# Eighteen places instead of twelve in the ring of the experts' loads, finer last loads of w_down, and the final scaling divided among three engines

## The chip, the cores and the metric

One core of a Trainium2 chip runs the kernel. The metric is device microseconds of one execution. The engines are named as in the profile: PE (matrix products), DVE (elementwise, from SBUF and PSUM), ACT (scaling and functions), POOL (elementwise on SBUF) and SP (only issues transfers). ACT and POOL can issue transfers too. All transfers run on the same 16 DMA engines of the core.

## What is computed

Two transformer blocks run one after the other on 256 tokens of width 1024, in 32-bit floats. The first holds a mixer of window attention, a recurrent scan and memory attention, and a convolutional feed-forward layer. The second holds two kinds of attention, and then a mixture of 32 experts, whose output is added to x before a last normalization:

```python
h2 = rmsnorm(x, norm2_g[l]) * (1.0 + sc2[:, None, :]) + sh2[:, None, :]
y_ffn = hierarchical_moe(h2, w_group[l], b_group[l], w_expert[l], b_expert[l],
                         w_gate[l], w_up[l], w_down[l])
x = x + g2[:, None, :] * y_ffn
...
return rmsnorm(x, final_g)
```

Each token goes to one of 4 groups and to 2 of the 8 experts of that group. An expert computes `silu(t @ w_gate) * (t @ w_up) @ w_down`, with w_gate and w_up of 1024 x 512 and w_down of 512 x 1024. Each of these matrices is 2 MB, so that the weights of all experts are 192 MB, and all of them are read.

## The kernel before

Everything up to the experts (called the front here) takes weights through a ring of six places of 1 MB each (`raw0` to `raw5`, 128 partitions x 2048 floats). `slot("raw")` (line 209) hands out the next place in turn. Each arriving MB is split into a high and a low part in a second ring `hi`, and PE multiplies with both parts.

The experts' stage begins at line 1431. Its ring has twelve places: two in the part `spare` of the long-lived tile `kept`, the six `raw`, and four new tiles `eraw0` to `eraw3` (`NMORE = 4`). `load` (line 1474) fills one place by one transfer of 1 MB, issued by SP (line 1479): four of the eight row groups of a gate or up matrix of one expert, or two of the four row groups of a down matrix. A load is behind all loads of the front in SP's queue (`issue_after(ahead)`), and it waits until the place's earlier content has been read. For an `eraw` tile that is the content of whichever tiles lay on the same bytes of SBUF before. Addresses are given out by an allocator that sees all tiles of the program, and a scheduler fixes the order of the instructions of each engine.

The loop runs over 8 groups of 4 experts (`EG = 4`). For each group, `times` loads four places for the first half of w_gate, multiplies, and does the same for the second half; then come both halves of w_up. `gather` (line 1442) builds the one-hot matrix `OH` and picks the tokens of the group into `XG` on PE (line 1454). `hidden` and `down` of the group before are done between the halves of the gate product. A group needs 24 loads, so that the whole stage has 192. In `times` the loop over the four row groups is outside of the loop over the experts, so that the four places of a half are all in use until its last products.

`down` (line 1504) loads two halves of w_down for four experts, and adds the products in two PSUM banks, `pd[0]` and `pd[1]` (columns 0 to 511 and 512 to 1023, line 1512). Then, for each half of the columns: DVE scales (`ye`, line 1518), ACT and DVE split into `yh` and `yl` (lines 1519 and 1520), PE brings the rows back to their tokens (lines 1523 and 1524), and DVE adds them to x (line 1525, one operand in PSUM and one in SBUF).

Three more transfers matter. The row `g2` is read after the loads of the front (line 234). The last gain goes to `row1` of `kept` (line 1584). `row0` of `kept` holds `g1`, which line 1288 reads for the last time ahead of the routing; `stage`, which lies right behind `row0`, is last used in the front.

`finish` (line 1586) makes the sums of squares (`squares`; three of four on ACT, the last on DVE, line 265), the reciprocal root on DVE (`token_rstd`, nine small instructions, lines 279 and 250 to 257), and then four products of 128 x 512 on DVE (line 1595), each followed by a store from SP (line 1596). After it stands a branch over `overflow`, which runs only where an expert has more than 32 tokens.

Of the kernel before, what the change touches and what calls it, by code (L numbers as in the profile page):

```python
# [9 lines left out]
F32 = mybir.dt.float32  # L10
# [4 lines left out]
AF = mybir.ActivationFunctionType  # L15
OP = mybir.AluOpType
# [4 lines left out]
D = 1024  # L21
NE = 32
CAP = 32
EG = 4
OC = 64
NMORE = 4
NRAW = 6
NHIS = 4
NEAR = 3
# [145 lines left out]
def _body(ctx, tc, nc, I, O, dbg):  # L175
    V, A, P, SY, G = nc.vector, nc.scalar, nc.tensor, nc.sync, nc.gpsimd

    def pool(stack, name, bufs=1, **kw):
        if kw.get("space") != bass.MemoryType.DRAM:
            kw["reuse_waits"] = "tile"  # L180
        return stack.enter_context(tc.tile_pool(name=name, bufs=bufs, **kw))
# [10 lines left out]
    kept = keep.tile([128, nk], F32, name="kept")  # L192
# [3 lines left out]
    x = pool(stx, "xs").tile([128, 2, D], F32, name="x")  # L196
# [12 lines left out]
    def slot(k):  # L209
        ring[k].append(ring[k].pop(0))  # L210
        return ring[k][-1]
# [29 lines left out]
    def pt(name="pt"):  # L241
        return psm.tile([128, 512], F32, name=name, tag="ps")

    def at(name="at"):
        return acc.tile([128, 512], F32, name=name, tag="acc")
# [13 lines left out]
    def squares(ssq, src, n):  # L259

        for t in range(2):
            junk = small.tile([128, 512], F32, name="junk", tag="junk", bufs=2)
            z = src[:, t, n * 512:n * 512 + 512]
            if n and t and SQ:
                V.scalar_tensor_tensor(junk, z, 1.0, z, op0=OP.mult, op1=OP.mult, accum_out=ssq[:, n, t:t + 1])
            else:
                A.activation(junk, z, AF.Square, accum_out=ssq[:, n, t:t + 1])

    def square_sums():
        return small.tile([128, 2, 2], F32, name="ssq", tag="ssq")  # L270
# [59 lines left out]
    def piece(srcs, J, behind=None, rest=(), first=0):  # L330


        w = sum(s.shape[-1] for s in srcs)
        out, n = [], max(1, 1024 // w)
        m = 2048 // (n * w) * n
        for i0 in range(first, J, m):
            i1 = min(J, i0 + m)
            rv = slot("raw")[:, :(i1 - i0) * w].rearrange("p (j f) -> p j f", f=w)
            c = 0
            for s in srcs:  # L340
                turn["load"] = SY.dma_start(rv[:, :, c:c + s.shape[-1]], s[:, i0:i1, :]).ins
                if behind is not None:
                    hold(turn["load"], behind)
                c += s.shape[-1]
            for j0 in range(i0, i1, n):
                k = min(n, i1 - j0)
                hl = slot("hi")
                hv, lv = (z[:, :k * w].rearrange("p (j f) -> p j f", j=k) for z in (hl[:, :1024], hl[:, 1024:]))
                rh = rv[:, j0 - i0:j0 - i0 + k, :]
                A.activation(hv, rh, AF.Copy)  # L350
                (G if j0 in rest else V).tensor_tensor(lv, rh, hv.bitcast(F32), op=OP.subtract)  # L351
                out.append((j0, k, hv, lv))
        return out
# [10 lines left out]
    def cols(w, a, b):  # L364
        return w.rearrange("(j p) n -> p j n", p=128)[:, :, a:b]
# [35 lines left out]
    def head_rstd(pl, src, n, tag):  # L401

        sq = pl.tile([128, n * 64], F32, name="hsq", tag="hsq", bufs=2)
        A.activation(sq, src, AF.Square)
        ss = small.tile([128, n], F32, name="hss", tag=f"hss{n}")
        V.tensor_reduce(ss, sq.rearrange("p (h d) -> p h d", d=64), axis=AX.X, op=OP.add)
        V.tensor_scalar(ss, ss, 1.0 / 64, 1e-6, op0=OP.mult, op1=OP.add)
        r = small.tile([128, n], F32, name=tag, tag=tag)
        rsqrt(r, ss, n)
        return r  # L410
# [54 lines left out]
    lo = ks["row1"][0]  # L465
# [29 lines left out]
    for c0, n in ((8, 2), (0, 4), (4, 4)):  # L495
        ws = piece([cols(w_in, 640 + c0 * 128, 640 + (c0 + n) * 128)], 8)
        for k, p in enumerate(feature_major(xs, ws, n)):
# [3 lines left out]
                                   op0=OP.mult, op1=OP.add)  # L501
# [6 lines left out]
    ws = piece([cols(w_in, 0, 512)], 8)  # L508
    for t, p in enumerate(token_major(xs, ws, 512)):
        r = head_rstd(pp, p, 8, "qkr")  # L510
# [3 lines left out]
    ws = piece([cols(w_in, 512, 640), cols(w_in, 1920, 2176)], 8)  # L514
    for t, p in enumerate(token_major(xs, ws, 384)):
        A.activation(va[:, t, :], p[:, :128], AF.Copy)
        r = head_rstd(pp, p[:, 128:384], 4, "qmr")
# [285 lines left out]
    ws = piece([cols(I["w_mem_kv"][0], 0, 512)], 8)  # L803
    for t, p in enumerate(token_major(ms_, ws, 512)):
        A.activation(mv[:, t, :], p[:, 256:], AF.Copy)
        r = head_rstd(pp, p[:, :256], 4, "mkr")
# [141 lines left out]
    ssq = square_sums()  # L948
    for n in range(2):
        ws = piece([cols(I["w_out"][0], n * 512, n * 512 + 512)], 8, behind=rw["near"])  # L950
# [21 lines left out]
    def conv(p, f):  # L972
        u = fp.tile([128, T], F32, name="conv", tag="conv", bufs=4)
        A.activation(u, p[:, :T], AF.Identity, scale=cw[:, 2, f:f + 1], bias=R("conv_b", f))
        V.scalar_tensor_tensor(u[:, 1:], p[:, :T - 1], cw[:, 1, f:f + 1], u[:, 1:], op0=OP.mult, op1=OP.add)
        V.scalar_tensor_tensor(u[:, 2:], p[:, :T - 2], cw[:, 0, f:f + 1], u[:, 2:], op0=OP.mult, op1=OP.add)
        return u

    for i in range(FB // 2):
        ws = piece([cols(w_up, 256 * i, 256 * i + 256), cols(w_up, 2816 + 256 * i, 2816 + 256 * i + 256)], 8)  # L980
        ps = [p[:, k * T:(k + 1) * T] for p in feature_major(xs, ws, 4, alloc=pt, each=2)
              for k in range(2)]
        for k in range(2):
            f = 2 * i + k
            g, v = conv(ps[k], f), conv(ps[2 + k], FB + f)
# [44 lines left out]
    ssq = square_sums()  # L1030
    for n in range(2):
        dst = None
        for off, J in ((0, 8), (8, 8), (16, 6)):
            ws = piece([w_down[off * 128:(off + J) * 128, n * 512:n * 512 + 512].rearrange("(j p) n -> p j n", p=128)], J)
# [217 lines left out]
    for m, _ in enumerate(project(1, "w_proj_diff_2")):  # L1252
        for k in range(0, 4, 2):
# [4 lines left out]
                                   op0=OP.mult, op1=OP.subtract)  # L1258
# [20 lines left out]
    ssq = square_sums()  # L1279
    for n in range(2):  # L1280
        ws = piece([cols(I["w_out_2"][0], n * 512, n * 512 + 512)], 8)
# [3 lines left out]
        for t, p in enumerate(ps):  # L1285
            f = slice(n * 512, n * 512 + 512)
            y = ip.tile([128, 512], F32, name="yo", tag="yo", bufs=2)
# [5 lines left out]
    ahead = turn["load"]  # L1293
# [77 lines left out]
    ep = pool(est0, "moe0")  # L1371
# [6 lines left out]
    r = token_rstd(x, ssq)  # L1378
# [39 lines left out]
    for t in range(2):  # L1418
# [3 lines left out]
    p = pt()  # L1422
# [8 lines left out]
    ep = pool(est, "moe")  # L1431
    lo = ks["spare"][0]
    ring["raw"] = ([kept[:, a:a + 2048] for a in (lo, lo + 2048)] + ring["raw"]
                   + [ep.tile([128, 2048], F32, name=f"eraw{i}") for i in range(NMORE)])
    wg, wu, wd = I["w_gate_2"][0], I["w_up_2"][0], I["w_down_2"][0]
    slots = C("slots")[:, :CAP]
    EC = EG * CAP
# [1 line left out]
    def quarter(e):  # L1439
        return slice(e * CAP, e * CAP + CAP)  # L1440
# [34 lines left out]
    def load(w, e, k0, n, k, d):  # L1475

        rv = slot("raw")[:, :n * d].rearrange("p (j f) -> p j f", f=d)
        with tc.issue_after(ahead):
            SY.dma_start(rv, w[e].rearrange("(p j) f -> p j f", j=k)[:, k0:k0 + n, :])
        return rv  # L1480
# [23 lines left out]
    def down(g, hT, back, iv):  # L1504
        pd = [at("pd") for _ in range(2)]
        for half in range(2):
            ws = [load(wd, EG * g + e, 2 * half, 2, 4, D) for e in range(EG)]
            for i in range(2):
                q = 2 * half + i
                for n in range(2):  # L1510
                    for e in range(EG):
                        P.matmul(pd[n][quarter(e), :], hT[:, q, quarter(e)], ws[e][:, i, n * 512:n * 512 + 512],  # L1512
                                 start=q == 0, stop=q == 3)
        for n in range(2):
            f = slice(n * 512, n * 512 + 512)
            y = ep.tile([128, 512], F32, name="ye", tag="ye", bufs=2)
            yh, yl = (ep.tile([128, 512], F32R, name=k, tag=k, bufs=2) for k in ("yh", "yl"))
            V.scalar_tensor_tensor(y, pd[n], iv, g2[:, f], op0=OP.mult, op1=OP.mult)  # L1518
            A.activation(yh, y, AF.Copy)  # L1519
            V.tensor_tensor(yl, y, yh.bitcast(F32), op=OP.subtract)  # L1520
            for t in range(2):
                p, b = pt(), back[:, t * 128:(t + 1) * 128]
                P.matmul(p, b, yh, start=True, stop=False)  # L1523
                P.matmul(p, b, yl, start=False, stop=True)  # L1524
                V.tensor_tensor(x[:, t, f], p, x[:, t, f], op=OP.add)
# [34 lines left out]
    NG = NE // EG  # L1560
# [22 lines left out]
    fg = part["row1"]  # L1583
    SY.dma_start(fg, I["final_g_2"][None, :].to_broadcast([128, D]))

    def finish(pl):
        ssq = square_sums()
        for n in range(2):
            squares(ssq, x, n)
        r = token_rstd(None, ssq)  # L1590
        for t in range(2):
            for n in range(2):
                f = slice(n * 512, n * 512 + 512)
                y = pl.tile([128, 512], F32, name="y", tag="y", bufs=4)
                V.scalar_tensor_tensor(y, x[:, t, f], r[:, t:t + 1], fg[:, f], op0=OP.mult, op1=OP.mult)
                SY.dma_start(O["out"][0, t * 128:(t + 1) * 128, f], y)

    finish(ep)
    ring["raw"] = list(raws)
    est.close()  # L1600
# [38 lines left out]
```

## Time and profile before

| | us |
|---|---|
| three timed runs, median (lowest to highest) | 1160.4 (1159.4 to 1164.57) |
| the profiled execution, own time | 1152.61 |
| its span, first to last instruction | 1150.6 |

| engine | busy us | share of the span |
|---|---|---|
| PE | 1008.5 | 88% |
| DVE | 486.8 | 42% |
| ACT | 363.1 | 32% |
| POOL | 32.5 | 3% |

The page of the profile gives the transfers' share and rate in 40 slices of 28.8 us. In slices 0 to 23 the rate is between 1 and 359 GB/s; from slice 24 on it is 420 to 422 GB/s in every slice but the last. The chain of work that ended last is put down to DMA for 28% of the span, to PE for 14% and to DVE for 2%. All times below are microseconds from the first instruction of the profiled execution.

### The profile page before, as it was taken

To read this page: it belongs to the slowest core of one execution; us is meant where nothing else is said; L and a number is where in the kernel's file an instruction comes from. 1 tells how busy PE (TensorE), PEld (TensorE's weight loads), DVE (VectorE), ACT (ScalarE), POOL (GpSimd) and SP (SyncE) were. 2 spreads that over 40 slices of the span, in tenths; PEclk is the share of its full clock that TensorE was granted. 3 is DMA by queue.
4 is the path that set the end of the run, shared out by engine and by line. 5 is a ranking of instruction groups with operands and counts; after the bars stand their busy time and mean duration, and the time that the engine had idled before them with its cause. 6 is when DMAs were issued, how large, how long until landed. Compare 5 with 4: busy or idle time off the path is not lost. (4 is left out here: it accounts for less than half of the span.)

```text
span 1150.6 us, 14934 instructions
## 1 busy us (share of the span) xinstructions
PE 1008.5 (88%) x6028; PEld 678.8 (59%) x6028; DVE 486.8 (42%) x1023; ACT 363.1 (32%) x647; POOL 32.5 (3%) x43
## 2 busy tenths in 40 slices
PE   5998989989999998999999988878787887878774
PEld 4984767659999986777999762423233231414121
DVE  5686533467888846547676720202020200101023
ACT  5553544146666644445554310000000000001001
POOL 0000010100000000211000000000000000000000
PEclk9999989999999998999999988999899998999888
DMA  9706375864567565353348549999999999999993
GB/s 359 252 1 186 140 303 174 286 204 134 184 183 226 183 220 183 121 172 111 119 139 327 203 176 420 421 421 421 421 421 421 422 421 420 422 420 421 421 420 140
DMA packets 94200, 317.49 MB, mean 276 GB/s; under 512 B 10730, under 2 KB 38048, under 8 KB 66348
## 3 DMA queue, kind: packets, MB, share of 16 engines
q1 hardware_dynamic: 90476, 291.25, 66.1%
q0 software_dynamic: 3648, 25.22, 5.9%
q8 instruction: 49, 0.80, 0.3%
q14 instruction: 27, 0.22, 0.1%
HBM read 315.36 MB, written 2.26 MB: 276 GB/s over the span
## 5 line engine op out<-in xcount | busy, mean ns | idle before, releaser
L351 DVE TENSOR_TENSOR hi<-raw,hi 128x1024 fp32r<-128x1024 f32 (+1 forms) x152 | 184.9, 1219 | 116.1 <-ACT hi L350 115.5
L350 ACT ACTIVATE hi<-raw 128x1024 fp32r<-128x1024 f32 (+1 forms) x152 | 159.6, 1054 | 165.6 <-PE at L380 87.1
L1518 DVE SCALAR_TENSOR_TENSOR ye<-pd,iv,kept 128x512 f32<-128x512 f32 x16 | 12.0, 750 | 281.0 <-PE pd L1512 280.1
L1512 PE MATMUL pd<-raw,hT 128*32 128x512 f32 x368 | 101.5, 599 | 19.4 <-DMA raw<-in_w_down_dram 18.7
L395 PE MATMUL pt<-fh,hi 128*128 128x256 f32 x352 | 99.7, 283 | 0.0
L397 PE MATMUL pt<-fh,hi 128*128 128x256 f32 x352 | 99.6, 283 | 0.0
L396 PE MATMUL pt<-fl,hi 128*128 128x256 f32 x352 | 99.6, 283 | 0.0
L1488 PE MATMUL pg<-eraw,XG 128*32 128x512 f32 x224 | 56.1, 771 | 26.0 <-DMA eraw<-in_w_gate_dram 26.0
L1512 PEld LDWEIGHTS pd<-raw,hT 128*32 128x32 f32 x368 | 23.4, 109 | 93.6 <-DMA raw<-in_w_down_dram 50.2
L1488 PE MATMUL pg<-raw,XG 128*32 128x512 f32 x272 | 58.3, 676 | 14.4 <-DMA raw<-in_w_gate_dram 14.4
L396 PEld LDWEIGHTS pt<-fl,hi 128*128 128x128 f32 x352 | 67.6, 192 | 0.0
L395 PEld LDWEIGHTS pt<-fh,hi 128*128 128x128 f32 x352 | 67.6, 192 | 0.0
L397 PEld LDWEIGHTS pt<-fh,hi 128*128 128x128 f32 x352 | 67.6, 192 | 0.0
L1454 PEld LDWEIGHTS pt<-OH,xa 128*128 128x128 f32 x256 | 62.0, 334 | 5.9 <-issue 5.0
L1454 PE MATMUL pt<-OH,xa 128*128 128x128 f32 x256 | 64.5, 409 | 0.7 <-DVE OH L1447 0.7
L1519 ACT ACTIVATE yh<-ye 128x512 fp32r<-128x512 f32 x16 | 10.1, 631 | 143.6 <-DVE ye L1518 143.6
L1494 DVE TENSOR_TENSOR h<-h,pu 128x512 f32<-128x512 f32 x8 | 5.5, 689 | 114.9 <-PE pu L1488 114.9
L1488 PEld LDWEIGHTS pg<-eraw,XG 128*32 128x32 f32 x224 | 11.3, 133 | 64.7 <-DMA eraw<-in_w_gate_dram 45.6
L1493 ACT ACTIVATE h<-pg 128x512 f32<-128x512 f32 x8 | 4.8, 597 | 128.8 <-PE pg L1488 128.8
L1488 PE MATMUL pu<-eraw,XG 128*32 128x512 f32 x256 | 43.6, 596 | 0.8 <-DMA eraw<-in_w_up_dram 0.8
L1512 PE MATMUL pd<-kept,hT 128*32 128x512 f32 x112 | 36.6, 605 | 4.8 <-ACT h L1493 4.8
L1488 PEld LDWEIGHTS pg<-raw,XG 128*32 128x32 f32 x272 | 12.2, 121 | 45.1 <-DMA raw<-in_w_gate_dram 26.2
(465 smaller groups left out, 2008.8 us busy)
## 6 DMA issues: line engine op xcount, KB each, us to landing
raw<-in_w_down_dram SPq DMA_DIRECT2D x56, 1024.0 KB, 19.8
raw<-in_w_gate_dram SPq DMA_DIRECT2D x34, 1024.0 KB, 19.5
eraw<-in_w_up_dram SPq DMA_DIRECT2D x32, 1024.0 KB, 19.6
eraw<-in_w_gate_dram SPq DMA_DIRECT2D x28, 1024.0 KB, 16.5
raw<-in_w_in_dram SPq DMA_DIRECT2D x27, 1024.0 KB, 5.1
kept<-in_w_ada_dram POOLq DMA_DIRECT2D x24, 1024.0 KB, 6.3
raw<-in_w_up_dram SPq DMA_DIRECT2D x44, 512.0 KB, 4.6
kept<-in_w_up_dram SPq DMA_DIRECT2D x16, 1024.0 KB, 19.6
```

The lines of the kernel that those rows point to most:

```text
L350: A.activation(hv, rh, AF.Copy)
L351: (G if j0 in rest else V).tensor_tensor(lv, rh, hv.bitcast(F32), op=OP.subtract)
L395: P.matmul(d, wh[:, j, f], xh[xj], start=i == 0 and j == 0 and k % each == 0, stop=False)
L396: P.matmul(d, wh[:, j, f], xl[xj], start=False, stop=False)
L397: P.matmul(d, wl[:, j, f], xh[xj], start=False, stop=i == len(ws) - 1 and j == n - 1 and k % each == each - 1)
L1454: P.matmul(pv[:, j, :], by_j(xa[:, t])[:, jj * 4 + j, :], OH[:, t], start=t == 0, stop=t == 1)
L1488: P.matmul(p[quarter(e), :], XG[:, jj, quarter(e)], ws[e][:, j, :], start=jj == 0, stop=jj == 7)
L1493: A.activation(h, pg, AF.Silu)
L1494: V.tensor_tensor(h, h, pu, op=OP.mult)
L1512: P.matmul(pd[n][quarter(e), :], hT[:, q, quarter(e)], ws[e][:, i, n * 512:n * 512 + 512], start=q == 0, stop=q == 3)
L1518: V.scalar_tensor_tensor(y, pd[n], iv, g2[:, f], op0=OP.mult, op1=OP.mult)
L1519: A.activation(yh, y, AF.Copy)
```

## The change

- `NMORE` goes from 4 to 9, so that there are five more `eraw` tiles, and the 1024 + 1024 floats of `row0` and `stage` become an eighteenth place, at the end of the ring. The ring's order is: two of `spare`, six `raw`, nine `eraw`, one of `row0` and `stage`.
- The last half of w_down of the last group comes in 12 transfers in place of 4: for each of the four experts 512 KB (its third row group), then for each 256 KB (the first 512 columns of its fourth row group), then for each the other 256 KB. Rows in memory are 4 KB and 2 KB long there, in place of 8 KB.
- In `finish`, POOL multiplies x with the last gain, in four pieces, while the sums of squares are made. Once the reciprocal root is there, DVE scales the two pieces of tokens 0 to 127 and ACT those of tokens 128 to 255, and SP and ACT each issue two of the four stores.

```diff
-NMORE = 4
+NMORE = 9
...
     ring["raw"] = ([kept[:, a:a + 2048] for a in (lo, lo + 2048)] + ring["raw"]
-                   + [ep.tile([128, 2048], F32, name=f"eraw{i}") for i in range(NMORE)])
+                   + [ep.tile([128, 2048], F32, name=f"eraw{i}") for i in range(NMORE)] + [kept[:, lo - 2048:lo]])
...
-            ws = [load(wd, EG * g + e, 2 * half, 2, 4, D) for e in range(EG)]
+            if g == NG - 1 and half:
+
+                ws = [slot("raw").rearrange("p (j f) -> p j f", f=D) for e in range(EG)]
+                for i, f in ((0, slice(0, D)), (1, slice(0, 512)), (1, slice(512, D))):
+                    for e in range(EG):
+                        with tc.issue_after(ahead):
+                            SY.dma_start(ws[e][:, i, f], wd[EG * g + e].rearrange("(p j) f -> p j f", j=4)[:, 2 + i, f])
+            else:
+                ws = [load(wd, EG * g + e, 2 * half, 2, 4, D) for e in range(EG)]
...
     def finish(pl):
-        ssq = square_sums()
+        ssq, y = square_sums(), {}
         for n in range(2):
+            f = slice(n * 512, n * 512 + 512)
+            for t in range(2):
+                y[t, n] = pl.tile([128, 512], F32, name="y", tag="y", bufs=4)
+                G.tensor_tensor(y[t, n], x[:, t, f], fg[:, f], op=OP.mult)
             squares(ssq, x, n)
         r = token_rstd(None, ssq)
-        for t in range(2):
-            for n in range(2):
-                f = slice(n * 512, n * 512 + 512)
-                y = pl.tile([128, 512], F32, name="y", tag="y", bufs=4)
-                V.scalar_tensor_tensor(y, x[:, t, f], r[:, t:t + 1], fg[:, f], op0=OP.mult, op1=OP.mult)
-                SY.dma_start(O["out"][0, t * 128:(t + 1) * 128, f], y)
+        for n in range(2):
+            for t in range(2):
+                if t:
+                    A.activation(y[t, n], y[t, n], AF.Copy, scale=r[:, t:t + 1])
+                else:
+                    V.tensor_scalar(y[t, n], y[t, n], r[:, t:t + 1], None, op0=OP.mult)
+                (A if t else SY).dma_start(O["out"][0, t * 128:(t + 1) * 128, n * 512:n * 512 + 512], y[t, n])
```

## Rows read from the trace of the kernel before

**Rows 1.** Windows: stretch, length, busy time by engine (instructions), PE clock, DMA share, GB/s.

```profile
24.00:28.00 4.00, 4.00 (x36) 4.00 (x35) 3.54 (x5) 2.71 (x5) 0.00 (x0) 1.00 1.05 388
656.00:662.00 6.00, 3.50 (x30) 3.15 (x29) 5.47 (x25) 2.50 (x5) 2.00 (x1) 0.89 0.25 87
662.00:678.00 16.00, 12.87 (x71) 9.99 (x71) 4.65 (x36) 1.53 (x5) 0.00 (x0) 0.72 0.09 34
680.00:700.00 20.00, 19.88 (x136) 11.57 (x125) 1.31 (x5) 4.05 (x6) 0.00 (x0) 1.00 1.01 420
900.00:1000.00 100.00, 84.30 (x415) 34.86 (x414) 13.00 (x26) 7.47 (x13) 0.00 (x0) 0.95 1.01 421
```

**Rows 2.** Timeline of SP's queue, 645 to 700: start, length, line, transfer.

```profile
646.88 0.33 SPq L1479 DMA_DIRECT2D raw<-in_w_gate_dram  x1
655.99 0.33 SPq L234 DMA_DIRECT2D kept<-ada_d  x1
661.70 0.33 SPq L1584 DMA_DIRECT2D kept<-in_final_g_dram  x1
678.09 0.80 SPq L1479 DMA_DIRECT2D kept<-in_w_up_dram  x2
```

**Rows 3.** Waits of SP's queue from 560 on: total, times, longest.

```profile
SPq L1479 <- PE pg L1488: 39.1, 21, 16.1
```

**Rows 4.** The chain that ended last, in order of time: start, length, what.

```profile
653.40 0.64 DVE yo L1288
...
674.50 3.57 PE pg L1488 x31
...
679.46 11.01 DMA raw<-in_w_up_dram
...
1111.14 19.93 DMA eraw<-in_w_down_dram
...
1131.12 3.63 PE pd L1512 x20
```

**Rows 5.** Timeline of PE: start, length, line, operation, idle before.

```profile
652.91 0.39 PE L380 MATMUL at<-hi,ml 128*128 128x512 f32 x1
...
657.88 1.98 PE L1276 MATMUL pt<-kept,xaT 128*128 128x40 f32 x16 [0.36 <-ACT xaT L1272]
...
1126.17 1.90 PE L1512 MATMUL pd<-eraw,hT 128*32 128x512 f32 x4 [0.58 <-DMA eraw<-in_w_down_dram]
```

**Rows 6.** DMA issues by line: count, KB each, median us from issue to landing.

```profile
raw<-in_w_down_dram SPq DMA_DIRECT2D x56, 1024.0 KB, 19.8
...
raw<-in_w_up_dram SPq DMA_DIRECT2D x44, 512.0 KB, 4.6
...
out_dram<-y SPq DMA_DIRECT2D x4, 256.0 KB, 3.1
```

**Rows 7.** Timeline of DVE and SP at the end.

```profile
1133.92 1.61 DVE L1518 SCALAR_TENSOR_TENSOR ye<-pd,iv,kept 128x512 f32<-128x512 f32 x2 [16.73 <-PE pd L1512]
...
1136.83 2.48 DVE L1525 TENSOR_TENSOR x<-pt,x 128x512 f32<-128x512 f32 x4
...
1139.35 0.69 DVE L265 SCALAR_TENSOR_TENSOR junk<-x 128x512 f32<-128x512 f32 x1
...
1141.93 2.74 DVE L1595 SCALAR_TENSOR_TENSOR y<-x,rstd,kept 128x512 f32<-128x512 f32 x4
1142.71 2.36 SPq L1596 DMA_DIRECT2D out_dram<-y  x4
```

**Rows 8.** POOL's products and DVE beside them: timelines, then line 1085's min/median/max ns.

```profile
659.68 2.00 POOL L1392 TENSOR_TENSOR xa<-xa,kept 128x1024 f32<-128x1024 f32 x1 [129.01 <-ACT xa L1391]
660.56 1.13 DVE L1532 TENSOR_TENSOR ge<-lg,gmx 128x8 f32<-128x8 f32 x1
663.18 0.15 DVE L1532 TENSOR_TENSOR ee<-ei,emx 128x16 f32<-128x16 f32 x1
L1085 POOL TENSOR_TENSOR r<-r,r x8: 1263/1743/2271, 470.4 to 528.5; 128x512 f32<-128x512 f32 x8
```

## The prediction

> **What bounds the kernel now.** I read the page's line of transfer rates first, then windows, then SP's queue, then the chain. From 680 on the 16 DMA engines are never free: 420 and 421 GB/s at a DMA share of 1.01, while PE has 84.3 us of work in 100 [rows 1]. A place of 1 MB (1.0486 MB) takes 1.0486 / 0.421 = 2.49 us, and the chain is DMA up to 1131.07, where the last load lands (1111.14 + 19.93) [rows 4]. So the experts' stage ends when the stream began plus what was then left, and only work ahead of the stream or behind it counts.
>
> Ahead of it stands a hole. The twelfth load is issued at 646.88, and the thirteenth only at 678.09 [rows 2]: it waits 16.1 us for PE's first gate product, which empties the first place [rows 3]. PE begins that product at 674.50, and the chain goes over to DMA at 679.46 [rows 4]. In between, the DMA share is 0.25 in 656 to 662 and 0.09 in 662 to 678 [rows 1], so that 6 x 0.75 + 16 x 0.91 = 19.1 us of transfer time lie idle after 656.
>
> **The ring.** Six more places let loads 13 to 18 go into the hole. The price of six loads is 6 x 2.49 = 14.9 us, and 19.1 us are there. Do they get in? What lay on the bytes must have been read. The candidates for the five new tiles are the buffers of the front's end: the split weights and merged activations, whose last product is at 652.91, and the transposed tokens of the router, whose last products run from 657.88 for 1.98 us, to 659.9 [rows 5]. `row0` is read last by line 1288, from 653.40 for 0.64 us [rows 4]. So all six can be issued by 660. SP issues one in some 0.4 us [rows 2], and all would be landed at 660 + some 2 + 14.9 = 677, ahead of 679.5. Even behind the two transfers that SP has in that time (`g2` at 655.99, the last gain at 661.70 [rows 2]) they end at 679, with the stream going on without a gap. In SP's queue stand behind the six: those two rows, needed only in `down` and in `finish`, and load 19.
>
> More than 14.9 us isn't to be had there: load 19 waits for the first gate product as load 13 did, and that hangs on the routing on DVE and on the gather, which no load touches. Nor should it be less later. PE starts with more loads in hand, works them off at 0.843 x 2.49 = 2.10 us a load [rows 1], and falls back to waiting for DMA where 674.5 + 2.10 n = 679.5 + 2.49 (n - 18), at about n = 102 of 192. Until then, loads 19 to 22 need the places that PE frees at 678, as now, and every later one has more room than with twelve. Term: -14.9, with bounds -14.9 and 0.
>
> **The finer last loads.** Now ten products stand behind the last landing: 20 records in 3.63 us [rows 4], two records to a product; two products of one expert alone took 1.90 us [rows 5], so one takes about 1.05. With pieces only the last expert's last product is left: 3.63 - 1.05 = 2.58, and as the first bank is complete about 2.5 us ahead (four pieces of 0.26 MB at 421 GB/s), its scaling and splitting run under the last landings. The way from the last product (1134.75) to the reciprocal root (start of line 1595, 1141.93 [rows 7]) holds two instructions of each kind on DVE; half of them go under. Counting `ye`, the split, PE's way back and two adds, this shortens the way by about 0.5. Terms: -2.6 and -0.5.
>
> Against it: eight issues more, and rows of 2 and 4 KB. In 24 to 28, with loads in rows of 2 KB about, the rate was 388 GB/s [rows 1]. The 4.19 MB at that rate cost 4.19 x (1/0.388 - 1/0.421) = 0.85 us; at the full rate 0. I take +0.4, the middle, since half of the bytes keep rows of 4 KB. The fixed part of a transfer is hidden as long as enough are in flight: a load of 1 MB lands 19.8 us after its issue [rows 6], which is eight at 2.49. Eight pieces are 2 to 4 MB, so 5 to 10 us, over the 4.6 us that a transfer of 512 KB takes to land [rows 6]. The Trainium skill speaks against this edit: "DMA: Bandwidth & Descriptors", section "Rules for kernel authors", wants at least 1 MiB per DMA, and its section "Anatomy of one DMA" puts some 2.0 us fixed on each; unhidden, eight more would be +16 us by that page.
>
> **The end.** Four products of 0.70 us in a row on DVE (2.74 in all [rows 7]) become two on DVE beside two on ACT, and two issue queues: 2 x 0.70 less, against one issue of 0.36 in between on ACT: -1.0. POOL's four products are meant to be hidden under the sums and the root. But they aren't free to DVE: while POOL multiplied from 659.68 to 661.68, a product of 128 x 8 took 1.13 us on DVE, to 661.69, and its like beside no POOL work 0.15 [rows 8]. DVE's instruction with two operands in SBUF waited until POOL was done. POOL needs at least 1.26 us for 128 x 512, 1.74 in the median [rows 8], so four need 5 to 7 us, from the first finished piece of x on. The adds of x take one operand from PSUM, but the split, the squares on DVE (1139.35) and the reciprocal root's chain up to 1141.93 [rows 7] do not. I expect two such waits of 1.05 on the path: +2.1. Bounds: 0 (the products fall between) and +3.8 (three at 1.26). On POOL and ACT nothing is queued behind but the branch. The stores' landing (3.1 [rows 6]) and what follows stay.
>
> **The sum.** -14.9 - 2.6 - 0.5 + 0.4 - 1.0 + 2.1 = -16.5. The profiled execution, 1152.6, would become 1136.1. It lies 7.8 under the median of the timed runs; I carry that difference over, so 1160.4 - 16.5 = 1143.9.
>
> One thing more has no row. The allocator deals all addresses anew with five more tiles, and which tile of the front waits for which may change. The nearest row is the wait of 16.1 us for a place [rows 3], the other end is none; as the front is ordered by its data, I take 0, with 3 us to either side. The forecast's own range is 1138 to 1148.
>
> **Rivals.**
> 1. *Only a part gets in.* If some tiles lie on bytes that are read until the gather ends at 674.5, their loads join the stream rather than the hole. Three of six give 7.5 less: 1151.4. For it: SBUF is nearly filled by the stage's tiles. Against: everything listed above is read by 660, and 3 us of spare time are left [rows 1, 5].
> 2. *It doesn't do what it says.* SP holds the six behind 678 altogether, say for the order in which the scheduler puts them. Then only the end's -1.6 is left: 1158.8. Against: now the loads are issued as soon as places are free.
> 3. *Slower: a load at the head of SP's queue waits.* SP issues in order. If one of loads 13 to 18 lies on bytes that group 0 still reads (`XG`, read until its last up product near 697, the end of the window that PE fills [rows 1]), all loads behind it stand. Each us past 679.5 costs one, each load ahead of it saves 2.49; from 679.5 + 1.6 + 5.8 = 687 on with none ahead it is slower by over 0.5%. At 697 with none ahead: 1160.4 + 17.5 - 1.6 = 1176.
> 4. *The last pieces pay their fixed part one by one.* 4.6 us to land for 512 KB, 1.25 of it moving [rows 6], leaves 3.4; eight more would give 27: 1143.9 + 27 = 1171. Against: 421 GB/s with eight in flight [rows 1, 6]. By the 2.0 us of the Trainium skill ("DMA: Bandwidth & Descriptors", section "Anatomy of one DMA") it would be about 1160.
>
> **How the numbers follow.** Forecast 0.74; part of it 0.13; none 0.06; head of the queue 0.04; fixed parts 0.03. What a measurement of this kernel can tell from no change is 0.5%, 5.8 us. Forecast and rival 1 lie beyond it: faster 0.87. Rival 2 is the same: 0.06. Rivals 3 and 4: slower 0.07. The range takes in the forecast with its bounds and most of rival 1: 1137.5 to 1152.5.
>
> **What would show it.** Right: eighteen loads issued by 662; DMA share near 1 from 656 to 678; the thirteenth to eighteenth landing there and load 19 issued at 678; the last landing near 1117; two records of PE behind it; DVE's small instructions after the squares stretched to about 1 us each time that a POOL product runs. Wrong: a first product later than 674.5, windows of the front that differ by over 3 us, gaps in the rate after 680, or a rate under 388 in the last 10 us of the stream.

## The result and the profile after

| | before | after |
|---|---|---|
| median of the timed runs, us | 1159.95 (4 runs, 1159.4 to 1164.57) | 1144.16 (4 runs, 1143.15 to 1149.26) |
| profiled execution, its own time, us | 1152.61 | 1143.15 |
| its span, us | 1150.6 | 1141.0 |
| issue of the first load behind the first gate product | 678.09 | 683.50 |
| from that issue to the end of the span | 472.5 | 457.5 |

The ratio is 0.9869, with a 95% interval of 0.9843 to 0.9896: 15.8 us less.

The two profiled executions are not alike ahead of the experts, though the program is the same there. Windows of before and then of after (stretch, length, busy time and instructions of PE, PEld, DVE, ACT, POOL, then PE clock, DMA share, GB/s):

```profile
220.00:230.00 10.00, 10.00 (x63) 6.12 (x56) 5.22 (x17) 2.08 (x4) 1.61 (x3) 1.00 0.77 263
```

```profile
220.00:230.00 10.00, 10.00 (x37) 6.91 (x36) 2.56 (x9) 0.52 (x1) 0.56 (x1) 0.50 0.50 180
```

PE was busy for the whole window, for the whole of 200 to 210, and for 9.57 of the 10 us between, in both. In after its granted clock was 0.88 in 210 to 220 and 0.50 here (the lower of its two levels, 1.2 GHz), and 37 of its records lie in the window instead of 63. By the starts of the same DVE instructions, after is 0.1 us late ahead of 210, 6.0 late at 240, and 5.4 late from 480 to the gate. All thirteen other profiles of this study, that of the kernel with twelve places and the new ends (experiment 2) too, have a granted clock of between 0.50 and 0.66 in this window; the profile of before on which the prediction rests is the exception. With twelve places, the kernel of experiment 2 has its gate 6.7 us later (684.76 against 678.09), which is most of the 7.8 us by which the profiled time of before lay under its own median. So kernels are compared below by the last line of the table, from the issue of the first load behind the first gate product (here called the gate) to the end of the span. It leaves that difference out.

**The hole.** Windows of after, answering to [rows 1]:

```profile
656.00:662.00 6.00, 5.49 (x39) 4.73 (x37) 4.52 (x8) 1.69 (x4) 0.00 (x0) 1.00 0.72 255
662.00:678.00 16.00, 10.38 (x56) 9.93 (x56) 9.53 (x57) 3.44 (x8) 1.99 (x1) 0.69 0.87 350
678.00:680.00 2.00, 2.00 (x13) 1.88 (x16) 0.00 (x0) 0.05 (x1) 0.00 (x0) 0.90 0.00 0
680.00:700.00 20.00, 20.00 (x146) 11.85 (x142) 0.97 (x6) 3.89 (x6) 0.00 (x0) 1.00 0.79 317
900.00:1000.00 100.00, 83.27 (x415) 34.43 (x414) 12.99 (x26) 7.47 (x13) 0.00 (x0) 0.93 1.01 421
```

The DMA share went from 0.25 to 0.72 in 656 to 662 and from 0.09 to 0.87 in 662 to 678. (The kernel of experiment 4, whose front is as late as that of after and whose six loads are held, has 0.36 and 0.18 there.) From about 677 to the gate, some 7 us, nothing moves: all eighteen places are full. Afterwards the rate is the same 421 GB/s.

The timeline of SP's queue in after, answering to [rows 2], shows the six added loads: the second of the row at 645.23 (issued at 650.6), and the five from 658.53 to 662.7. They stand ahead of the two rows for `g2` and the last gain:

```profile
645.23 5.70 SPq L1479 DMA_DIRECT2D eraw<-in_w_up_dram  x2
652.30 0.33 SPq L1479 DMA_DIRECT2D raw<-in_w_gate_dram  x1
658.53 2.96 SPq L1479 DMA_DIRECT2D eraw<-in_w_up_dram  x3
661.58 0.60 SPq L1479 DMA_DIRECT2D eraw<-in_w_gate_dram  x1
662.23 0.43 SPq L1479 DMA_DIRECT2D kept<-in_w_gate_dram  x1
662.75 0.60 SPq L234 DMA_DIRECT2D kept<-ada_d  x1
667.11 0.33 SPq L1592 DMA_DIRECT2D kept<-in_final_g_dram  x1
683.50 0.80 SPq L1479 DMA_DIRECT2D kept<-in_w_gate_dram  x2
```

**The end.** The chain of after, answering to [rows 4 and 7] (start, length, what):

```profile
1114.24 6.30 DMA eraw<-in_w_down_dram
1120.54 0.76 DVE ye L1526
...
1122.01 0.73 PE pt L1531 x2
...
1123.23 0.98 PE pd L1520 x2
1124.63 0.99 PE pd L1520 x2
1125.65 0.76 DVE ye L1526
...
1129.76 1.10 DVE junk L265 x2
1130.97 0.86 DVE ms L279
```

The last two products `pd` (two records each) now stand between home products `pt` of the first half of the columns, and the two DVE steps at the end of this piece are longer than before. Both are taken up below.

### The profile page after: what moved, and what is told of

Same layout as the page of the kernel before. It is cut to its first block, busy times and chain, and to the rows that moved or that the text cites. A ratio compares the mean times of both kernels' runs of the same rounds, so it can differ in the third digit from the quotient of the medians.

```text
span 1141.0 us, 14968 instructions
## 1 busy us (share of the span) xinstructions
PE 1005.3 (88%) x6028; PEld 682.4 (60%) x6028; DVE 486.1 (43%) x1021; ACT 364.6 (32%) x649; POOL 37.3 (3%) x47
## 5 line engine op out<-in xcount | busy, mean ns | idle before, releaser
L1520 PE MATMUL pd<-eraw,hT 128*32 128x512 f32 x256 | 71.8, 600 | 10.7 <-DMA eraw<-in_w_down_dram 9.3
L1520 PE MATMUL pd<-raw,hT 128*32 128x512 f32 x176 | 48.6, 599 | 7.9 <-DMA raw<-in_w_down_dram 5.7
L1488 PE MATMUL pg<-raw,XG 128*32 128x512 f32 x208 | 39.4, 629 | 12.8 <-DMA raw<-in_w_gate_dram 12.8
L1520 PEld LDWEIGHTS pd<-eraw,hT 128*32 128x32 f32 x256 | 17.3, 109 | 55.8 <-DMA eraw<-in_w_down_dram 28.8
L1488 PE MATMUL pu<-eraw,XG 128*32 128x512 f32 x296 | 49.1, 595 | 0.0
L481 PE MATMUL ada<-kept 128*32 128x512 f32 (+1 forms) x216 | 33.4, 633 | 5.5 <-DMA kept<-in_w_ada_dram 5.5
L380 PE MATMUL at<-hi,il 128*128 128x512 f32 x96 | 38.1, 397 | 0.0
```

Source lines behind the costliest of these rows:

```text
L380: P.matmul(d, xl[xj][:, ts], wh[:, j, :], start=False, stop=last)
L481: P.matmul(p[32 * g:32 * g + 32, :], ones[0:1, :32] if j == 8 else ca[:, j:j + 1].to_broadcast([128, 32]), w[:, g * 512:(g + 1) * 512], st ...
L1488: P.matmul(p[quarter(e), :], XG[:, jj, quarter(e)], ws[e][:, j, :], start=jj == 0, stop=jj == 7)
```

## The experiments

All of them by the stretch from the gate to the end, and within it at two points: where `pd[1]` is complete (end of the last `pd` product, or start of the `ye` that waits for it) and where the final scaling starts.

| kernel | gate | to `pd[1]` complete | to scaling | to the end | median of timed runs |
|---|---|---|---|---|---|
| before | 678.09 | 456.7 | 463.8 | 472.5 | 1159.95 |
| ends only (e2) | 684.76 | | | 472.5 | 1159.27 |
| six loads held (e4) | 685.24 | | | 472.6 | 1159.78 |
| fifteen places (e3) | 685.29 | | | 464.9 | 1152.21 |
| ring only (e1, e10) | 685.66, 683.49 | 441.7 (e10) | 448.9 (e10) | 457.4, 457.4 | 1148.8, 1144.36 |
| the change (first, e9, e12) | 683.50, 684.32, 684.82 | 442.15 (first) | 450.0 (first) | 457.5, 457.6, 457.6 | 1144.16, 1144.68, 1144.55 |
| home products last (e5) | 690.35 | 439.7 | 448.5 | 456.05 | 1148.17 (one run) |
| POOL one half (e6) | 684.96 | 442.15 | 448.8 | 457.7 | 1144.58 (one run) |
| both (e8) | 684.25 | 439.7 | 447.3 | 456.05 | 1145.09 |
| both, POOL put later (e11) | 684.39 | 439.6 | 447.2 | 455.5 | 1142.16 |
| both, POOL waits (e13) | 684.83 | 439.6 | 446.9 | 455.3 | 1142.95 |

**1. The ring alone.** The kernel before with

```diff
-NMORE = 4
+NMORE = 9
...
-                   + [ep.tile([128, 2048], F32, name=f"eraw{i}") for i in range(NMORE)])
+                   + [ep.tile([128, 2048], F32, name=f"eraw{i}") for i in range(NMORE)] + [kept[:, lo - 2048:lo]])
```

> Only the ring of the change: eighteen places; the last loads of w_down come as 1 MB each and the final scaling stays on DVE, as before. Theory (the hole): loads 13 to 18 go into the idle time ahead of the first gate product, and the ring alone is worth 6 x 2.49 = 14.9 us: 1145.0, ratio 0.987; in the trace no load between the eighteenth and the first gate product, a rate of 420 us-long stretches as before, and 19.5 us from the last landing to the end, as before. Rival (the end carries a good part): the ring gives under 12, the rest is the finer loads' and the shared scaling's: over 1148.

457.4 from the gate, as the theory of the hole has it; the whole gain of the change is there. The median of 1148.8 (ratio 0.9914, 0.9897 to 0.993) seemed to say otherwise, so it was run again, below (8).

**2. The ends alone.** The changed kernel with `NMORE = 4` and without the place in `kept`.

> Twelve places as before, with the change's finer last loads and its shared final scaling. Theory (PE's order takes the gain of the finer loads): two of the last products stand in PE's queue behind the way home of the first half of the columns, so from the last landing to the end it takes 18.9 us against 19.5 before, and the pieces land 0.5 late: no more than -0.2 in all, 1159.8, not to be told from no change. Rival (the sum of the prediction): -1.6, 1158.3, with 17.5 us from the last landing to the end.

472.5, as before; ratio 1.0004 (0.998 to 1.0028). Finer loads and shared scaling bring nothing by themselves.

**3. Fifteen places.** The changed kernel with `NMORE = 7` and without the place in `kept`.

> The change with three new places fewer: fifteen in all (seven eraw, without the place of row0 and stage). Theory (the hole): each place ahead of the first product is worth 2.49 us, so three give 7.5 and half of the gain is lost: 1152.0, ratio 0.993. Rival (depth): a deeper ring helps because loads stand clear of PE's stalls in the stream, and fifteen places are as good as eighteen or nearly: under 1147.

464.9: 7.6 under 472.5 for three places and 7.5 over 457.4 for the next three; ratio 0.995 (0.9921 to 0.9979). The gain is 2.5 us a place.

**4. Eighteen places, the six loads held.** The changed kernel, with loads 13 to 18 waiting for the first gate product:

```diff
+        turn["n"] = turn.get("n", 0) + 1
...
+            z = SY.dma_start(rv, w[e].rearrange("(p j) f -> p j f", j=k)[:, k0:k0 + n, :]).ins
+        if 12 < turn["n"] <= 18:
+            hold(z, turn["first"])
...
+        turn.setdefault("first", z)
```

> The change with eighteen places, but loads 13 to 18 are held until PE has finished the first gate product of group 0, as load 13 is by its place with twelve places. Theory (the hole): nothing is left of the ring's gain: 1159.7, within 0.3 percent of the kernel before, though each later load has eighteen places. Rival (depth): the deeper ring keeps most of its worth: under 1150.

472.6; ratio 1.0 (0.998 to 1.0021). The windows of this kernel show the hole open again:

```profile
656.00:662.00 6.00, 5.49 (x30) 4.46 (x28) 2.85 (x5) 1.43 (x4) 0.00 (x0) 1.00 0.36 146
662.00:678.00 16.00, 10.37 (x64) 9.91 (x64) 11.23 (x61) 3.13 (x9) 1.99 (x1) 0.75 0.18 66
```

So the number of places is worth nothing later in the stage; what counts is that six loads move ahead of the gate.

**5. Home products behind the last products.** In the changed kernel, in `down`, PE's home products are put behind the last `pd` product of each expert:

```diff
+                        turn["pd", e] = P.matmul(pd[n][quarter(e), :], hT[:, q, quarter(e)],
...
-                P.matmul(p, b, yh, start=True, stop=False)
-                P.matmul(p, b, yl, start=False, stop=True)
+                with ExitStack() as behind:
+                    for e in range(EG):
+                        behind.enter_context(tc.issue_after(turn["pd", e]))
+                    P.matmul(p, b, yh, start=True, stop=False)
+                    P.matmul(p, b, yl, start=False, stop=True)
```

> The change, with PE's products of the way home in every group queued behind that group's last product of w_down. It is the same work. Theory (PE's order): now two of the last eight products of the second half of the columns stand behind the way home of the first half, and the second bank is complete 3.5 us after the last landing; in this order it is complete 1.1 to 1.3 us after it, and from the issue of load 19 to the end of the span it takes 455.1 us in place of 457.5. Rival (the pieces' landing or DVE sets the end, PE's order doesn't): 457 or more. A part may be lost where POOL's products of the first half of the columns move behind the second half's work on DVE: 456.

In the timeline of PE in the changed kernel the last two products `pd` stand between the steps of the first half's way home, whose first step waits for ACT's `yh`. Their pieces had landed at 1121.4 and 1122.0:

```profile
1122.01 0.73 PE L1531 MATMUL pt<-yh,back 128*128 128x512 f32 x2 [0.18 <-ACT yh L1527]
1122.73 0.50 PE L1532 MATMUL pt<-yl,back 128*128 128x512 f32 x1
1123.16 1.04 PE L1520 MATMUL pd<-eraw,hT 128*32 128x512 f32 x2
1124.14 0.49 PE L1532 MATMUL pt<-yl,back 128*128 128x512 f32 x1
1124.56 1.04 PE L1520 MATMUL pd<-eraw,hT 128*32 128x512 f32 x2
```

With the edit the products run in a row:

```profile
1121.68 8.36 PE L1520 MATMUL pd<-eraw,hT 128*32 128x512 f32 x27
1129.98 0.50 PE L1534 MATMUL pt<-yh,back 128*128 128x512 f32 x1
```

and `pd[1]` is complete 2.4 us earlier from the gate (442.15 to 439.7). Of that 0.9 is given back on the way home, so that the end comes 1.5 earlier. The one timed run, 1148.17, says nothing here: its gate came 5.5 us or more later than in the profiles of the change. The timeline of DVE in this kernel shows where:

```profile
1130.75 1.28 DVE L1536 TENSOR_TENSOR x<-pt,x 128x512 f32<-128x512 f32 x2
1131.95 1.26 DVE L1528 TENSOR_TENSOR yl<-ye,yh 128x512 fp32r<-128x512 f32 x1
```

The second half's `yl` now waits behind the first half's additions, and takes 1.26 instead of 0.69, because POOL's products of the first half (from 1131.57) run beside it.

**6. POOL multiplies only the first half.** ACT scales both pieces of that half and issues their stores, and DVE makes the other two by the old product of three operands, for SP to store:

```diff
+                if n == 0:
-                G.tensor_tensor(y[t, n], x[:, t, f], fg[:, f], op=OP.mult)
+                    G.tensor_tensor(y[t, n], x[:, t, f], fg[:, f], op=OP.mult)
...
-                if t:
+                if n == 0:
...
-                    V.tensor_scalar(y[t, n], y[t, n], r[:, t:t + 1], None, op0=OP.mult)
-                (A if t else SY).dma_start(O["out"][0, t * 128:(t + 1) * 128, n * 512:n * 512 + 512], y[t, n])
+                    V.scalar_tensor_tensor(y[t, n], x[:, t, f], r[:, t:t + 1], fg[:, f], op0=OP.mult, op1=OP.mult)
+                (SY if n else A).dma_start(O["out"][0, t * 128:(t + 1) * 128, n * 512:n * 512 + 512], y[t, n])
```

> The change, with POOL multiplying only the two pieces of the first half of the columns; the other two are made on DVE in one instruction each, as in the kernel before, and ACT scales POOL's two. Theory (POOL holds DVE up): the last squares on DVE take 0.69 us again in place of 1.10 and the first small instruction 0.16 in place of 0.85, the reciprocal root is there 1.1 us sooner, and from load 19 to the end it takes 456.6 in place of 457.5, as two products of 0.70 on DVE take 0.4 more than two of 0.48. Rival (those two instructions are long for another cause): they stay at 1.1 and 0.85, and it takes 457.5 or more.

Timelines of DVE and POOL in the changed kernel, then of DVE in this one:

```profile
1124.67 0.69 DVE L1533 TENSOR_TENSOR x<-pt,x 128x512 f32<-128x512 f32 x1 [0.71 <-PE pt L1532]
1129.76 1.08 DVE L265 SCALAR_TENSOR_TENSOR junk<-x 128x512 f32<-128x512 f32 x1
1130.97 0.85 DVE L279 SCALAR_TENSOR_TENSOR ms<-ssq 128x2 f32<-128x2 f32 x1
1124.04 1.09 POOL L1600 TENSOR_TENSOR y<-x,kept 128x512 f32<-128x512 f32 x1 [456.96 <-DVE x L1533]
1129.21 2.58 POOL L1600 TENSOR_TENSOR y<-x,kept 128x512 f32<-128x512 f32 x2 [2.62 <-DVE x L1533]
```

```profile
1131.22 0.69 DVE L265 SCALAR_TENSOR_TENSOR junk<-x 128x512 f32<-128x512 f32 x1
1132.02 0.16 DVE L279 SCALAR_TENSOR_TENSOR ms<-ssq 128x2 f32<-128x2 f32 x1
```

The square falls from 1.08 to 0.69 and the small instruction behind it from 0.85 to 0.16: 1.1 us of hold, gone, and the scaling starts 1.2 us earlier from the gate (450.0 to 448.8). An addition to x with one operand in PSUM took 0.69 in the changed kernel although a POOL product (1124.04 to 1125.13) ran beside its first 0.46. This is the rule of the Trainium skill, "SBUF — State Buffer", section "SBUF: two separate sides": DVE and POOL share a pair of ports, and of an instruction of DVE with two inputs in SBUF and one of POOL that reads SBUF, the one that starts first has the pair for its whole length while the other waits. The rows agree: the small instruction ends at 1131.82, as POOL's second product does (1131.79), and POOL's two products, with the square between them, took 2.58, against 2.14 in the version of 9.

The end doesn't come earlier, though: 457.7. From the start of the scaling to the end it is 8.9 here and 7.5 in the changed kernel. DVE's two products take 1.42 instead of 0.88, and SP issues its second store 1.44 behind the start of the scaling instead of 0.96. The last store of all is issued only 0.1 later (1.44 against 1.36, which was ACT's), so most of the 1.4 comes behind the issues; its cause was not settled.

**7. Both, and the change beside it.** The edits of 5 and 6 together, with the changed kernel run again in the same set.

> Both edits in one: the way home behind the last products on PE, and POOL with the first half of the columns only. Theory: the two gains add up: 454.2 us from load 19 to the end in place of 457.5, and 3 us less than the changed kernel in time: 1141, ratio to the kernel before 0.984. Rival: one of the two waits takes the place of the other, 455.5 or more.

> The changed kernel once more, beside the one before and the version with both edits, on one chip. Theory: 1144 to 1146, ratio 0.986 to 0.988; 457.5 us from load 19 to the end of the span, whatever the front takes in this execution.

456.05 against 457.6, where 454.2 was expected: up to the scaling the two edits add up to 2.7 (450.0 to 447.3), as their sum (2.4 and 1.2, less the 0.9 of POOL and DVE on the way home), but the slower finish of 6 takes 1.2 back. By whole times, 1145.09 and 1144.68, the two cannot be told apart.

**8. Ring alone once more, with the change on the same chip.** 

> The kernel before with the ring edit alone (eighteen places, no finer loads, the old finish), beside the changed kernel on the same chip. What is open: by whole times the ring alone took 1148.8 us and the changed kernel 1144.7 us, in different sets of runs, which would put 4 us on the finer loads and the finish; by the stretch from the issue of the first load behind the first gate product to the end they are 457.4 and 457.5 us, which puts nothing there. Theory (the ends are worth nothing, and the whole times differed by how long TensorE was held at a granted clock of 0.50 ahead of that load): the stretch is 457.4 again and the whole times of the two kernels lie within 2.5 us of each other. Rival (the ends are worth what the whole times say): 4 us longer than the changed kernel here too.

> The changed kernel again, for the two kernels beside it. Stretch from the issue of the first load behind the first gate product to the end: 457.5 us by either theory; whole time within 2.5 us of the ring alone if the ends are worth nothing, 4 us below it if they are worth what the earlier whole times say.

1144.36 for the ring alone (ratio 0.986, 0.9836 to 0.9884) and 1144.55 for the whole change (0.9858, 0.9834 to 0.9882); from the gate 457.4 and 457.6. The ends are worth nothing, and the 4 us between the earlier sets were not theirs. The last row of `pd` in the ring alone starts at 438.0 from the gate, where PE's wait for the last load ends:

```profile
1121.53 3.62 PE L1512 MATMUL pd<-eraw,hT 128*32 128x512 f32 x20 [0.58 <-DMA eraw<-in_w_down_dram]
```

In the changed kernel the last piece is issued at 1116.9 and lands 5.2 us later (the least of its twelve), at 1122.0, which is 438.5 from the gate.

**9. POOL's half behind `yl`.** The version of 7, with POOL's two products put behind the second half's `yl`: first by the order of issue alone (e11), then by a wait (e13):

```diff
-                    G.tensor_tensor(y[t, n], x[:, t, f], fg[:, f], op=OP.mult)
+                    z = G.tensor_tensor(y[t, n], x[:, t, f], fg[:, f], op=OP.mult).ins
+                    if pl is ep:
+                        hold(z, turn["yl"])
```

> The version with the products home behind the last products and POOL multiplying only the first half; added to it, POOL's two products of the first half wait for the subtraction that makes the second half's yl on DVE. There that subtraction took 1.26 us beside POOL against 0.69 without it. Theory (POOL's product holds DVE's operation with two inputs in SBUF): yl is back at 0.69, POOL's two products end before the last square, and the stretch from the issue of the first load behind the first gate product to the end is 456.05 - 0.5 = 455.5 us. Rival (yl was late by DVE's own two additions ahead of it): yl's start moves by nothing and the stretch stays at 456.0; and a loss of up to 0.4 us if the held products now run beside the last square, which took 1.08 us beside POOL and 0.69 without it.

> In the version before this one the order asked of POOL was no wait: its first product began 0.4 us ahead of yl, as without it. Here POOL's two products of the first half truly wait for the end of the subtraction that makes the second half's yl on DVE. Theory (POOL's product holds DVE's operation with two inputs in SBUF, and did so to yl): yl is back at 0.69 from 1.25, the two products take 1.09 each and end within 0.2 us of the start of the last square on DVE, and the stretch from the issue of the first load behind the first gate product to the end goes from 456.05 to some 455.6 us; whole time about 1142. Rival (yl was long for another reason, its data or its own engine): yl stays at 1.25 and the stretch at 456.0. Third: the second of the held products reaches into the last square, which then takes up to 1.08 instead of 0.69, and the stretch stays at 456.0 though yl is short.

The order of issue held nothing: POOL began 441.1 from the gate, as in 7, and `yl` stayed at 1.25. The stretch was nevertheless 0.5 shorter, all of it behind the scaling; that says how far this part of it varies, and nothing on `yl`. With the wait the theory held. Timelines of DVE and POOL in e13:

```profile
1126.28 0.68 DVE L1528 TENSOR_TENSOR yl<-ye,yh 128x512 fp32r<-128x512 f32 x1
1127.55 1.29 DVE L1536 TENSOR_TENSOR x<-pt,x 128x512 f32<-128x512 f32 x2 [0.59 <-PE pt L1535]
1128.87 0.99 DVE L265 SCALAR_TENSOR_TENSOR junk<-x 128x512 f32<-128x512 f32 x1
1127.18 2.14 POOL L1604 TENSOR_TENSOR y<-x,kept 128x512 f32<-128x512 f32 x2 [458.78 <-PE pt L1534]
```

`yl` is back at 0.68. POOL's second product ends at 1129.32, 0.45 into the square, which takes 0.99 instead of 0.69, as the third case had it, though the stretch did not stay at 456.0. The two additions keep their 1.29 with POOL beside them all the way. The scaling starts at 446.9, 3.1 ahead of the changed kernel, and the end comes 2.2 to 2.3 earlier (455.3 against 457.5 and 457.6). This is the shortest stretch of all; its median of 1142.95 (ratio 0.9833, 0.9809 to 0.9857) lies below the change's three medians, which were taken in other sets, with intervals that overlap.

A nineteenth place, for which 7 us of idle transfer time are left, was not measured.

## Why the prediction was right

Forecast 1143.9, measured 1144.16: the forecast's case, in the range. The terms of the sum, each from the gate:

| term | predicted | measured | from |
|---|---|---|---|
| ring | -14.9 | -15.0 | `pd[1]` complete 456.7 to 441.7, ring alone; 7.6 for the first three places |
| finer last loads, products behind the last landing | -2.6 | -0.1 | 3.7 us behind it in the ring alone, 3.6 in the change |
| pieces' slower rows | +0.4 | +0.55 | last landing at 438.0 and 438.5 |
| way home half under the landings | -0.5 | -0.55 | `pd[1]` to scaling 7.2 in the ring alone, 6.7 with POOL one half |
| POOL's hold on DVE | +2.1 (0 to 3.8) | +1.15 | 6.7 with POOL one half, 7.85 in the change |
| finish | -1.0 | -1.0 | scaling to end 8.5 in the ring alone, 7.5 in the change |
| sum | -16.5 | -14.95 | 472.5 to 457.5 or 457.6 |

**The ring** was right in its mechanism and its size. All six loads were issued by 662.7, ahead of the gate, and were moved by about 677; the places bring 2.5 us each while they fill the hole (3), and nothing where they don't (4). Rivals 1 (a part of them), 2 (none) and 3 (head of SP's queue) are out by the queue's rows and by 457.4. No part of the gain was given back behind it, as the prediction said of PE.

**The step that failed** is "With pieces only the last expert's last product is left". The pieces were there in time; PE was not free for them. The scheduler had put the last two products between the home products of the first half, and PE took them up in that order: the first home product at 1122.01, when ACT had made `yh`, and the last `pd` at 1124.56, 2.5 us after its piece had landed. So 3.6 us passed from the last landing to `pd[1]`, against 3.7 in the ring alone, and the term of -2.6 came to -0.1. The prediction counted the scaling and splitting of the first bank as work under the landings, and did not look at where its last two steps, on PE itself, would stand in PE's order. With the order mended, `pd[1]` is complete 1.1 after the last landing (5), as the prediction's 1.05 had it, and 2.4 us are won there.

**POOL's hold** was right in its mechanism and twice too large. Two waits were expected at 1.05 each; there were two, of 0.39 and 0.69, because a POOL product takes 1.09 us with no DVE work in its way, where the rows of before gave 1.26 at least [rows 8], and because DVE's instruction came when part of it was past. The two errors, 2.5 too hopeful and 0.95 too careful, make the 1.6 by which the sum was off.

**The finish** has the size that was forecast, but not for the reason given. Scaling and issues of the stores in the ring alone, then in the change:

```profile
1132.38 2.74 DVE L1595 SCALAR_TENSOR_TENSOR y<-x,rstd,kept 128x512 f32<-128x512 f32 x4
1133.16 2.32 SPq L1596 DMA_DIRECT2D out_dram<-y  x4
```

```profile
1133.48 1.33 ACT L1606 ACTIVATE y<-y,rstd 128x512 f32<-128x512 f32 x2 [3.59 <-DVE rstd L257]
1134.01 0.82 SPq L1609 DMA_DIRECT2D out_dram<-y  x2
1134.23 0.95 ACTq L1609 DMA_DIRECT2D out_dram<-y  x2
```

The last store is issued 1.4 behind the start of the scaling instead of 2.8, as the sum had it. But that store lands 4.3 after its issue instead of 2.9, so that its landing is 5.7 behind the start of the scaling in both. The 1.0 lies behind the landing, 1.8 to the end instead of 2.8, where the prediction had said that nothing changes. Why the end comes sooner there is not shown; that the number agrees is luck.

**Pieces and their fixed part** (rival 4). Eight more transfers cost 0.55 us, not 27 and not 16. Windows of the changed kernel over its last loads:

```profile
1100.00:1112.00 12.00, 8.51 (x47) 2.31 (x50) 0.69 (x1) 0.60 (x1) 0.00 (x0) 0.86 1.01 417
1112.00:1118.00 6.00, 6.00 (x37) 1.94 (x30) 0.00 (x0) 0.00 (x0) 0.00 (x0) 1.00 1.02 383
```

The rate falls to 383 GB/s at a share of 1.02: the engines are not idle between the pieces. The pieces land 1.29 and 0.65 us apart, which is some 407 and 402 GB/s. Of the rule of the Trainium skill ("DMA: Bandwidth & Descriptors", section "Rules for kernel authors") that wants 1 MiB a transfer for the most bandwidth, this is all that shows here, with eight transfers in flight. Nor do the fixed 2.0 us of the Trainium skill (same page, section "Anatomy of one DMA") add up along a full queue; the page gives them for transfers issued from POOL, and these are issued from SP.

**The offset of 7.8 us** between the profiled execution and the median was carried over. For a forecast of the median that is sound; but the changed kernel's own profiled time, which the same sum put at 1136.1, was 1143.15, since the profile of before was the fast exception and that of the change was not. A sum that is 1.6 too hopeful would have given 1145.5 for the median. The fourth timed run puts the median of before 0.45 lower, and the other 0.9 is little beside the spread of the change's own runs (1143.15 to 1149.26). That 0.3 us separates forecast and median is therefore luck; that the size is 15 us is not.

Of what the prediction named as wrong signs, a first product later than 674.5 (679.84 here) and windows of the front that differ by over 3 us came about. They do not come from the eighteen places: the kernel of experiment 2, with twelve, has its gate at 684.76. A rate under 388 in the last 10 us came about too (306 in 1112 to 1122), but before has 364 in 1120 to 1130, its own last stretch, so the sign does not tell pieces from whole loads. The last landing came at 1122.0 and not near 1117, by the later front.

## What to carry to other kernels

In a stage that is bound by one stream of transfers, first look for the time in which the stream stands still ahead of it, and price each buffer that lets a load into it at one load's transfer time, up to the length of that gap; elsewhere the deeper ring brought nothing here. Before work behind the last landing is called short, follow the consuming engine's queue in its order: finer pieces gave 0.1 us here while the products that eat them stood behind another chain, and 2.4 more without it. A term that comes out in number may still have come by another way, as the finish did. Where executions differ ahead of the changed stage, compare from an event that both kernels have, and run what is to be compared in one set.

## What the runs showed of the hardware

- POOL's product of 128 x 512 takes 1.09 us where no DVE instruction with two SBUF operands is in its way, and held such instructions for 0.3 to 0.69 us each; DVE's additions with one operand in PSUM kept their 0.69 beside it.
- Transfers of 512 and 256 KB in rows of 4 and 2 KB, eight in flight, moved at 383 GB/s in the window 1112 to 1118 and some 400 by their landings, against 421 for 1 MB.
- In 220 to 230 PE's granted clock was 1.00 in one execution and 0.50 to 0.66 in thirteen others, with PE busy for 9.57 us or more in all of them and the program of the front the same. In the profile of the change this put 6.0 us between it and before. The gates lie at 678.09 in the one and at 683.49 to 685.66 in the others, once at 690.35, where 0.50 to 0.58 lasted from 210 to 240; up to 3.6 us of these differences (ring alone, first profile) was there ahead of this window.
- From the start of the scaling to the end it took 8.5 us in the ring alone, 7.5 in the change, and 8.3 to 8.9 in the versions in which DVE made two of the pieces from x. The last store lands 5.7 us behind that start in the first two, so their difference lies behind the landing; its cause was not settled.
